# Recurrence gates and key products moved between ScalarE, VectorE and GpSimd in a two-layer hybrid backbone

## The chip, the cores and the metric

The kernel runs on one core of a Trainium2 chip. The metric is the device time of one execution in microseconds. Three runs of the kernel before took 1477.03, 1477.29 and 1481.97 us (median 1477.29 us). The engines are named as the profile names them: PE is TensorE, DVE is VectorE, ACT is ScalarE, POOL is GpSimd, SP issues the DMAs.

## The reference

Two layers work on 256 latent tokens `x` and 256 context tokens `ctx`, each 1024 wide, in fp32. A layer normalises, projects once, and feeds three mixers: a Fourier mix, windowed attention, and a gated linear recurrence that runs forward and backward over the tokens. The branches are gated, summed and projected, and a squared-ReLU MLP follows. What matters here is the recurrence. Cut to its core it computes, for 4 heads of 128 key channels:

```python
def hgrn_forget(z, lb):                 # gates of one direction
    k = (1.0 - lb) * sigmoid(-z)        # key
    f = sigmoid(z) + lb * sigmoid(-z)   # forget factor (the reference keeps its logarithm)
    return k, log(f)

def gla_chunked(q, k, v, logf, s0):     # o_t = q_t . S_t,  S_t = f_t * S_{t-1} + k_t v_t^T
    ...

def hgrn_bidir(q, kf, lff, kb, lfb, v, s_f, s_b):
    o_f, s_f_new = gla_chunked(q, kf, v, lff, s_f)
    o_b, s_b_new = gla_chunked(flip(q), flip(kb), flip(v), flip(lfb), s_b)
    return o_f + flip(o_b), s_f_new, s_b_new
```

With `lb` the lower bound, `f = (1 - lb) * sigmoid(z) + lb`: a sigmoid and an affine form with one factor and one summand per channel.

## The kernel before, in words

Large matrix products make up nearly all of PE's program. Weights arrive by DMA as tiles `raw` (128 x 1024 elements), are split into a high part `wh` (ACT, line 105) and a low part `wl` (DVE, line 108), and each product is done three times (`ws_group`, lines 275 to 277; `xs_group`, lines 291 to 293). The products of these lines need nothing of the recurrence until its branch is merged; between the recurrence's small products they are the fillers of PE's queue. The order on each engine is written by a scheduler when the program is built and stays fixed on the chip: an engine whose next instruction has to wait does not go on to a later one.

The recurrence is `hgrn(s, p)`, for the context (s = 0) and then the latent tokens (s = 1), and for two pairs of heads p, whose instructions alternate. Channels lie on partitions and the 256 tokens of two heads and both directions along the free axis. In the last layer the context has no queries and only makes its final states.

- The gates: `zt` holds the raw gates of both directions. ACT makes `sigmoid(-z)` into `wa` and `sigmoid(z)` in place. For each direction and head, line 877 (through `affine`, line 122) turns `zt` into the forget factors, 128 x 256 at a time, on DVE; lines 884 and following scale the keys into the tile `wk`, whose halves are `kop` and `ko`.
- The start of a pair: POOL multiplies the query with its sigmoid (line 890), DVE forms `wq` (the query times the factors, 128 x 1024), POOL forms a sum of keys (line 896), and PE makes the products inside a token (L866).
- A loop over h = 1, 2, 4, ..., 64, 128 joins neighbouring blocks of h tokens. At each level PE multiplies keys with queries (L866, L925 and L926 at the last), DVE masks the result into `cd`, multiplies the queries `wq` (line 931), and the keys are multiplied by the neighbouring block's decay. Up to h = 64 the keys of a pair take four instructions: two outer products into `wb` on DVE (lines 934 to 936, 128 x 128 each), a copy of the middle part on ACT (line 938), and one inner product on POOL (line 939, 128 x 256). `wb` and `wk` change places at each level. The next level's decays `z`, `t` are a product of this level's (line 948).
- For the context, PE then transposes the keys (L964) and multiplies them with the values (L973) into the states; L988 makes the output.

Of the kernel before, what the change touches and what calls it, by code (L numbers as in the profile page):

```python
# [15 lines left out]
AF = mybir.ActivationFunctionType  # L16
ALU = mybir.AluOpType
# [24 lines left out]
def _view(a, offset, dims):  # L42
    return bass.AP(tensor=a.tensor, offset=a.offset + offset, ap=[list(a.ap[0])] + [list(x) for x in dims])
# [3 lines left out]
def kernel(ctx: ExitStack, tc: tile.TileContext, io, dbg=None, stop=None):  # L47
    nc = tc.nc
# [11 lines left out]
    def sb(tag, shape, dtype=F32):  # L60
        uid[0] += 1
        return pool.tile(shape, dtype, tag=tag, name=f"{tag}{uid[0]}", bufs=BUFS[tag])

    def ps(tag, shape=(P, 512)):
        uid[0] += 1
        return psum.tile(list(shape), F32, tag=tag, name=f"{tag}{uid[0]}", bufs=PBUFS[tag])
# [7 lines left out]
    def act_cost(n):  # L74
        return 100 + 0.83 * n

    def dve_cost(n):
        return 70 + 1.04 * n

    def act(out, in_, func, cost=None, **kw):  # L80
        load["act"] += act_cost(out.free_size())
        return nc.scalar.activation(out=out, in_=in_, func=func, **kw)  # L82

    def tt(out, in0, in1, op):
        load["dve"] += dve_cost(out.free_size())
        return nc.vector.tensor_tensor(out=out, in0=in0, in1=in1, op=op)  # L86
# [5 lines left out]
    def evac(out, in_):  # L92
        n = out.free_size()
        top = max(load.values())
        for k in load:
            load[k] = max(load[k], top - 3000)
        if load["act"] + act_cost(n) < load["dve"] + dve_cost(n):
            load["act"] += act_cost(n)
            nc.scalar.copy(out=out, in_=in_)
        else:  # L100
            load["dve"] += dve_cost(n)
            nc.vector.tensor_copy(out=out, in_=in_)
# [18 lines left out]
    def affine(out, in_, mul, add):  # L121
        nc.vector.tensor_scalar(out=out, in0=in_, scalar1=mul, scalar2=add, op0=ALU.mult, op1=ALU.add)
# [292 lines left out]
    lbf = const.tile([P, DEPTH, 8], F32, name="lbf")  # L415
    oml = const.tile([P, DEPTH, 8], F32, name="oml")
# [148 lines left out]
    def layer(l):  # L565
# [278 lines left out]
        def hgrn(s, p):  # L844
# [4 lines left out]
            zt = z[s, p]  # L849
            k2 = sb("wk", [P, 2, 2, T])  # L850
            kop, ko = k2[:, 0], k2[:, 1]
            knew = sb("wb", [P, 2, T])
# [3 lines left out]
            def diag(c0, n):  # L856

                return _view(at, c0, [(512 + P, 2), (T, 2), (1, n)])

            def blocks(o, keys, n, queries):  # L860

                for j in range(2):
                    for hh in range(2):
                        for b in range(P // n):
                            t0 = j * P + b * n
                            nc.tensor.matmul(o[b * n:(b + 1) * n, j, hh, :], keys[:, hh, t0:t0 + n], queries(hh, t0, b),  # L866
                                             start=True, stop=True, tile_position=(0, b * n))
# [5 lines left out]
            for dr in range(2):  # L873
                for hh in range(2):
                    c = (1 - dr) * 4 + p * 2 + hh

                    affine(zt[:, dr, hh], zt[:, dr, hh], oml[:, l, c:c + 1], lbf[:, l, c:c + 1])
                    pair = sms[dr][:, hh].rearrange("p (n e) -> p n e", e=2)
                    if dr == 1:
                        outs = ((_view(k2, hh * T, [(2, P), (513, 2)]), pair),)  # L880
                    else:
                        outs = ((ko[:, hh, 0:T:2], pair[:, :, 0]), (kop[:, hh, 1:T:2], pair[:, :, 1]))
                    for o_, i_ in outs:
                        nc.vector.tensor_scalar(out=o_, in0=i_, scalar1=oml[:, l, c:c + 1], scalar2=None, op0=ALU.mult)
                        load["dve"] += dve_cost(128)
# [15 lines left out]
            tl, toff, n = zt, 0, 512  # L901
            t2l = sb("t2", [P, 2, 256])
            yield
            for li, h in enumerate(LEVELS + (128,)):
                nb = n // 2
                if doq and h < 32:
                    lv = ps("lv", (P, 2, 2, 32))
                    blocks(lv, kop, 32, lambda hh, t0, b: _view(q2, hh * T + t0, [(2 * h, 16 // h), (512 + h, 2), (1, h)]))
                    nc.vector.copy_predicated(cd, lmask[:, li, :].unsqueeze(1).unsqueeze(1).to_broadcast([P, 2, 2, 32]), lv)
                    load["dve"] += 200  # L910
                    if h == 16:
                        for b in range(4):
                            bs = slice(32 * b, 32 * b + 32)
                            nc.gpsimd.tensor_copy(out=diag(32 * b, 32)[bs], in_=cd[bs])
                elif doq and h < 128:

                    lv = ps("lv", (P, 2, 2, h))
                    blocks(lv, kop, h, lambda hh, t0, b: q2[:, 1 - b % 2, hh, t0 + (h, -h)[b % 2]:t0 + (2 * h, 0)[b % 2]])
                    for b in range(P // h):
                        bs = slice(h * b, h * b + h)  # L920
                        evac(diag(h * (b ^ 1), h)[bs], lv[bs])
                elif doq:
                    lv = ps("lv", (P, 2, 2, P))
                    for hh in range(2):
                        nc.tensor.matmul(lv[:, 0, hh, :], kop[:, hh, 0:P], q2[:, 1, hh, P:T], start=True, stop=True)  # L925
                        nc.tensor.matmul(lv[:, 1, hh, :], kop[:, hh, P:T], q2[:, 0, hh, 0:P], start=True, stop=True)  # L926
                    evac(_view(at, P, [(512 - P, 2), (T, 2), (1, P)]), lv)

                if doq and not (h == 128 and s == 0):
                    qv = _view(q2, 0, [(2 * h, nb), (512 + h, 2), (1, h)])  # L930
                    tt(qv, qv, _view(tl, toff + 1, [(2, nb), (n - 1, 2), (0, h)]), ALU.mult)
                if h < 128:
                    nq = nb // 2
                    for off, toff2 in ((0, n + 1), (3 * h, 2)):
                        tt(_view(knew, off, [(4 * h, nq), (1, h)]), _view(kop, off, [(4 * h, nq), (1, h)]),
                           _view(tl, toff + toff2, [(4, nq), (0, h)]), ALU.mult)
                    mid = [(4 * h, nq), (h, 2), (1, h)]
                    act(_view(knew, h, [(4 * h, nq), (1, 2 * h)]), _view(ko, h, [(4 * h, nq), (1, 2 * h)]), AF.Copy)
                    nc.gpsimd.tensor_tensor(out=_view(ko, h, mid), in0=_view(kop, h, mid),
                                            in1=_view(tl, toff, [(4, nq), (n + 3, 2), (0, h)]), op=ALU.mult)  # L940
                    kop, knew = knew, kop
                    if h == 1:
                        nt, noff = t2l, 0
                    elif h == 2:
                        nt, noff = zt, 0
                    else:
                        nt, noff = zt, toff + 2 * n
                    tt(_view(nt, noff, [(nb, 2), (1, nb)]), _view(tl, toff, [(n, 2), (2, nb)]),
                       _view(tl, toff + 1, [(n, 2), (2, nb)]), ALU.mult)
                    tl, toff, n = nt, noff, nb  # L950
                elif s == 0:
                    for off, toff2 in ((0, n + 1), (P, 0)):
                        kv_ = _view(kop, off, [(T, 2), (1, P)])
                        tt(kv_, kv_, _view(tl, toff + toff2, [(2, 2), (0, P)]), ALU.mult)
                yield
            dump(f"at{l}{s}{p}", at if doq else k2)
            if s == 0:
# [11 lines left out]
                for dr in range(2):  # L969
                    for hh in range(2):  # L970
                        c = (p * 2 + hh) * P
# [6 lines left out]
            if doq:  # L978
                o = ps("lv", (P, 2, 2, P))
                for i in range(2):  # L980
                    for hh in range(2):
                        c = (p * 2 + hh) * P
# [9 lines left out]
        for s in range(2):  # L992
            live = [hgrn(s, p) for p in range(2)]
            while live:
                live = [g for g in live if next(g, live) is not live]
# [378 lines left out]
```

## Time and profile before

| | |
|---|---|
| median of three runs | 1477.29 us |
| the profiled execution | 1479.77 us |
| its span in the trace | 1478.0 us |
| busy PE, DVE, ACT, POOL | 1442.6, 884.0, 663.9, 132.9 us |
| stretches of the recurrence, layer 0 | 215 to 262 us (context), 300 to 346 us (latent) |
| stretches of the recurrence, layer 1 | 1078 to 1112 us (context), 1112 to 1166 us (latent) |

A busy time is the sum over an engine's instructions on one execution. "PEclk" is the share of TensorE's full clock that was granted in a stretch: 1.00 is 2.4 GHz all the time, and a part of the stretch at 1.2 GHz lowers it. A wait is put down to the instruction that released it. The profiled execution took 1.8 us more than its span.

### The profile page before, as it was taken

To read this page: it belongs to the slowest core of one execution; us is meant where nothing else is said; L and a number is where in the kernel's file an instruction comes from. 1 tells how busy PE (TensorE), PEld (TensorE's weight loads), DVE (VectorE), ACT (ScalarE), POOL (GpSimd) and SP (SyncE) were. 2 spreads that over 40 slices of the span, in tenths; PEclk is the share of its full clock that TensorE was granted. 3 is DMA by queue.
4 is the path that set the end of the run, shared out by engine and by line. 5 is a ranking of instruction groups with operands and counts; after the bars stand their busy time and mean duration, and the time that the engine had idled before them with its cause. 6 is when DMAs were issued, how large, how long until landed. Compare 5 with 4: busy or idle time off the path is not lost.

```text
span 1478.0 us, 26336 instructions
## 1 busy us (share of the span) xinstructions
PE 1442.6 (98%) x10631; PEld 1253.1 (85%) x10632; DVE 884.0 (60%) x1783; ACT 663.9 (45%) x1220; POOL 132.9 (9%) x134
## 2 busy tenths in 40 slices
PE   7999998999999999999999999999998999999999
PEld 5887987888777788877777778998987999999998
DVE  4555759697334457433434334675788866766664
ACT  5454574454223346313223224464674545555544
POOL 3100003251000001000000000010055300000000
PEclk9999999999999999999999999999998999999999
DMA  9632212214466545455555533343223345656653
GB/s 309 223 95 63 72 58 69 73 42 132 159 214 199 171 129 158 141 166 174 173 169 173 171 114 101 87 119 100 61 81 102 115 143 174 197 159 199 187 184 115
DMA packets 178122, 205.83 MB, mean 139 GB/s; under 512 B 6800, under 2 KB 166320, under 8 KB 177488
## 3 DMA queue, kind: packets, MB, share of 16 engines
q1 hardware_dynamic: 177232, 201.44, 43.9%
q0 software_dynamic: 576, 2.62, 0.7%
q8 instruction: 83, 1.36, 0.4%
q14 instruction: 39, 0.32, 0.1%
q10 hardware_dynamic: 192, 0.08, 0.0%
HBM read 200.97 MB, written 3.15 MB: 138 GB/s over the span
## 4 chain that ended last, share of the span: by engine, by line
PE 83%; issue 8%; DVE 6%; POOL 1%; ACT 1%; SPq 1%; DMA 0%; DVEq 0%; ACTq 0%; POOLq 0%
PE mm L275 16%; PE mm L277 16%; PE mm L276 16%; PE tp L276 3%; PE tp L275 3%; PE tp L277 3%; PE lv L197 3%; PE lv L275 3%; PE lv L277 3%; PE lv L276 3%; PE mm L291 2%; PE mm L293 2%; PE mm L292 2%; DVE wq L86 1%; PE mm L512 1%
## 5 line engine op out<-in xcount | busy, mean ns | idle before, releaser
L86 DVE TENSOR_TENSOR wl<-raw,wh 128x1024 fp32r<-128x1024 f32 (+1 forms) x274 | 335.9, 1227 | 214.2 <-ACT wh L82 203.9
L82 ACT ACTIVATE wh<-raw 128x1024 fp32r<-128x1024 f32 (+1 forms) x278 | 290.3, 1047 | 350.0 <-PE mm L276 114.4
L275 PE MATMUL mm<-h,wh 128*128 128x512 f32 (+1 forms) x704 | 252.8, 359 | 1.3 <-DVE z L86 0.8
L277 PE MATMUL mm<-h,wl 128*128 128x512 f32 (+1 forms) x704 | 251.0, 357 | 1.9 <-DVE wl L86 1.9
L276 PE MATMUL mm<-h,wh 128*128 128x512 f32 (+1 forms) x704 | 250.5, 356 | 0.0
L275 PEld LDWEIGHTS mm<-h,wh 128*128 128x128 f32 x704 | 134.4, 191 | 34.6 <-ACT wh L82 6.7
L277 PEld LDWEIGHTS mm<-h,wl 128*128 128x128 f32 x704 | 134.4, 191 | 21.0 <-DVE wl L86 2.4
L276 PEld LDWEIGHTS mm<-h,wh 128*128 128x128 f32 x704 | 134.4, 191 | 19.3 <-issue 1.8
L291 PE MATMUL mm<-wh,h 128*128 128x256 f32 x384 | 112.2, 292 | 0.3 <-DVE xm L86 0.3
L293 PE MATMUL mm<-wh,h 128*128 128x256 f32 x384 | 110.6, 288 | 0.0
L292 PE MATMUL mm<-wl,h 128*128 128x256 f32 x384 | 109.6, 285 | 0.0
L275 PE MATMUL mm<-br,wh 128*128 128x258 f32 (+2 forms) x325 | 103.0, 317 | 0.2 <-DVE xm L86 0.2
L276 PE MATMUL mm<-br,wh 128*128 128x258 f32 (+2 forms) x325 | 103.1, 318 | 0.0
L277 PE MATMUL mm<-br,wl 128*128 128x258 f32 (+2 forms) x325 | 102.8, 317 | 0.0
L275 PE MATMUL mm<-z,wh 128*128 128x256 f32 (+1 forms) x272 | 89.0, 330 | 0.0
L276 PE MATMUL mm<-r,wh 128*128 128x256 f32 (+1 forms) x272 | 88.6, 327 | 0.0
L277 PE MATMUL mm<-z,wl 128*128 128x256 f32 (+1 forms) x272 | 88.4, 327 | 0.0
L90 DVE SCALAR_TENSOR_TENSOR xm<-mm,modT,xm 128x256 f32<-128x256 f32 x76 | 34.5, 480 | 76.5 <-PE mm L277 76.4
L291 PEld LDWEIGHTS mm<-wh,h 128*128 128x128 f32 x384 | 73.8, 192 | 1.2 <-DVE xm L86 0.4
L293 PEld LDWEIGHTS mm<-wh,h 128*128 128x128 f32 x384 | 74.0, 193 | 0.6 <-issue 0.3
L292 PEld LDWEIGHTS mm<-wl,h 128*128 128x128 f32 x384 | 73.9, 193 | 0.3
L82 ACT ACTIVATE g<-mm 128x512 f32<-128x512 f32 (+1 forms) x48 | 24.8, 516 | 102.5 <-PE mm L277 102.2
(363 smaller groups left out, 3123.2 us busy)
## 6 DMA issues: line engine op xcount, KB each, us to landing
raw<-in_w_ff SPq DMA_DIRECT2D x128, 512.0 KB, 4.1
raw<-in_w_in SPq DMA_DIRECT2D x106, 512.0 KB, 3.7
raw<-in_w_branch SPq DMA_DIRECT2D x24, 512.0 KB, 3.4
wa<-in_w_mod SPq DMA_DIRECT2D x24, 512.0 KB, 6.2
br<-in_w_mod SPq DMA_DIRECT2D x24, 512.0 KB, 5.7
wk<-in_w_mod SPq DMA_DIRECT2D x16, 512.0 KB, 4.5
wq<-in_w_mod SPq DMA_DIRECT2D x16, 512.0 KB, 6.4
raw<-in_w_out SPq DMA_DIRECT2D x16, 512.0 KB, 3.4
```

Of the source, the lines that this page charges most:

```text
L82: return nc.scalar.activation(out=out, in_=in_, func=func, **kw)
L86: return nc.vector.tensor_tensor(out=out, in0=in0, in1=in1, op=op)
L90: return nc.vector.scalar_tensor_tensor(out=out, in0=in0, scalar=scalar, in1=in1, op0=op0, op1=op1)
L197: nc.tensor.matmul(total[n][32 * j:32 * j + 32, :], cT[:, kt, :], raws[i][j // 2][:, j % 2, :], start=(kt == 0), stop=(kt == 7), tile_posi ...
L275: nc.tensor.matmul(o, w(0, kt, cs), act_h(kt)[:, c0:c1], start=(kt == 0), stop=False)
L276: nc.tensor.matmul(o, w(0, kt, cs), act_l(kt)[:, c0:c1], start=False, stop=False)
L277: nc.tensor.matmul(o, w(1, kt, cs), act_h(kt)[:, c0:c1], start=False, stop=(kt == nk - 1))
L291: nc.tensor.matmul(o, act_h(kt)[:, ts], w(0, kt, cs), start=(kt == 0), stop=False)
L292: nc.tensor.matmul(o, act_h(kt)[:, ts], w(1, kt, cs), start=False, stop=False)
L293: nc.tensor.matmul(o, act_l(kt)[:, ts], w(0, kt, cs), start=False, stop=(kt == 7))
L512: o = nc.tensor.matmul(sums[ch][t // 2][:, (t % 2) * T:(t % 2 + 1) * T], h[a_][d // 4][:, d % 4, ts], wt[ch, d // 4][w_][:, d % 4, :], sta ...
```

## The change

Three edits in `hgrn`. The affine form of the gates becomes an ACT activation (Identity with a factor and a summand per partition) in place of DVE's tensor_scalar. The two outer key products of a level become one DVE instruction of 128 x 256, whose views take the first and last block of each four. The inner key product goes from POOL to DVE.

```diff
-                    affine(zt[:, dr, hh], zt[:, dr, hh], oml[:, l, c:c + 1], lbf[:, l, c:c + 1])
+                    act(zt[:, dr, hh], zt[:, dr, hh], AF.Identity, scale=oml[:, l, c:c + 1], bias=lbf[:, l, c:c + 1])
...
-                    for off, toff2 in ((0, n + 1), (3 * h, 2)):
-                        tt(_view(knew, off, [(4 * h, nq), (1, h)]), _view(kop, off, [(4 * h, nq), (1, h)]),
-                           _view(tl, toff + toff2, [(4, nq), (0, h)]), ALU.mult)
+                    ends = [(4 * h, nq), (3 * h, 2), (1, h)]
+                    tt(_view(knew, 0, ends), _view(kop, 0, ends), _view(tl, toff + n + 1, [(4, nq), (1 - n, 2), (0, h)]), ALU.mult)
                     mid = [(4 * h, nq), (h, 2), (1, h)]
                     act(_view(knew, h, [(4 * h, nq), (1, 2 * h)]), _view(ko, h, [(4 * h, nq), (1, 2 * h)]), AF.Copy)
-                    nc.gpsimd.tensor_tensor(out=_view(ko, h, mid), in0=_view(kop, h, mid),
-                                            in1=_view(tl, toff, [(4, nq), (n + 3, 2), (0, h)]), op=ALU.mult)
+                    tt(_view(ko, h, mid), _view(kop, h, mid), _view(tl, toff, [(4, nq), (n + 3, 2), (0, h)]), ALU.mult)
```

In the program, 32 tensor_scalars leave DVE and 32 activations come to ACT; 112 outer products become 56; 56 inner products leave POOL and come to DVE. The scheduler also writes other orders around them. Line numbers behind the edit are smaller by 2, so that L964 of before is L962 of the change.

First place, PE at the start of layer 0's recurrence. `tp` from `a` is the end of the attention; `lv` from `r` and `t` are the products inside a token, `lv` from `wq` and `wk` those of the first level, and `mm` the large products. Before:

```order
L803 MATMUL tp_1698<-a_1612,a_797 64x128 x8
L803 MATMUL tp_1698<-a_1655,a_797 64x128
L866 MATMUL lv_2376<-r_1721,t_2374 32x32 x9
L803 MATMUL tp_1698<-a_1655,a_797 64x128 x7
L866 MATMUL lv_2376<-r_1721,t_2374 32x32 x7
L866 MATMUL lv_2419<-r_1721,t_2417 32x32 x16
L866 MATMUL lv_2439<-wq_2372,wk_2353 32x32 x16
L866 MATMUL lv_2463<-wq_2415,wk_2396 32x32 x16
```

With the change, where the line of dots leaves out 23 more large products:

```order
L803 MATMUL tp_1698<-a_1612,a_797 64x128 x8
L803 MATMUL tp_1698<-a_1655,a_797 64x128
L866 MATMUL lv_2376<-r_1721,t_2374 32x32 x16
L277 MATMUL mm_3471<-h_101,wl_3442 128x512
...
L277 MATMUL mm_3509<-h_101,wl_3506 128x512
L803 MATMUL tp_1698<-a_1655,a_797 64x128 x7
L866 MATMUL lv_2419<-r_1721,t_2417 32x32 x16
L866 MATMUL lv_2439<-wq_2372,wk_2353 32x32 x16
L866 MATMUL lv_2462<-wq_2415,wk_2396 32x32 x16
```

25 large products of 512 columns now stand between the first pair's products inside a token and the first level's.

Second place, DVE at the same start; `z_1717` and `z_1718` are the gates of the two pairs, `wk_2353` and `wk_2396` their keys. Before:

```order
L884 TENSOR_SCALAR wk_2396<-wa_2398,oml 128x128x2 x2
L122 TENSOR_SCALAR z_1717<-z_1717,oml,lbf 128x256 x4
L122 TENSOR_SCALAR z_1718<-z_1718,oml,lbf 128x256 x4
L86 TENSOR_TENSOR wb_2354<-wk_2353,z_1717 128x128 x2
L86 TENSOR_TENSOR wb_2397<-wk_2396,z_1718 128x128 x2
L86 TENSOR_TENSOR wq_2372<-r_1721,z_1717 128x1024
L86 TENSOR_TENSOR wl_3592<-raw_3589,wh_3591 128x1024
L86 TENSOR_TENSOR wq_2415<-r_1721,z_1718 128x1024
```

With the change:

```order
L884 TENSOR_SCALAR wk_2396<-wa_2398,oml 128x128x2 x2
L86 TENSOR_TENSOR wq_2372<-r_1721,z_1717 128x1024
L86 TENSOR_TENSOR wb_2354<-wk_2353,z_1717 128x128x2
L86 TENSOR_TENSOR wk_2353<-wk_2353,z_1717 128x128x2
L86 TENSOR_TENSOR wb_2397<-wk_2396,z_1718 128x128x2
L102 COPY cd<-lv_2376 128x128
L86 TENSOR_TENSOR t_2395<-z_1717 128x512
L86 TENSOR_TENSOR wl_3564<-raw_3561,wh_3563 128x1024
L86 TENSOR_TENSOR wk_2396<-wk_2396,z_1718 128x128x2
L86 TENSOR_TENSOR wq_2415<-r_1721,z_1718 128x1024
```

The eight affine instructions are gone, the first `wq` stands at the head, and the inner key products (`wk` from `wk`) stand among the rest.

Third place, PE in layer 1 where the context's keys are transposed for the states (`tp` from `ident` and `wb` or `wk`). Before:

```order
L275 MATMUL mm_10964<-h_8497,wh_10960 128x256
L276 MATMUL mm_10964<-h_8499,wh_10960 128x256
L277 MATMUL mm_10964<-h_8497,wl_10961 128x256
L964 MATMUL tp_10303<-ident,wb_10196 128x128
L964 MATMUL tp_10303<-ident,wk_10195 128x128
```

With the change:

```order
L277 MATMUL mm_11044<-br_9009,wl_11027 128x256
L275 MATMUL mm_11044<-br_9009,wh_11026 128x256
L276 MATMUL mm_11044<-br_9010,wh_11026 128x256
L962 MATMUL tp_10261<-ident,wb_10168 128x128
L962 MATMUL tp_10261<-ident,wk_10167 128x128
```

The transposes moved behind 99 more large products of 256 columns, from the gates' products (`h`) into those of the first merged branch (`br`).

## Rows read from the trace of the kernel before

**Rows 1.** The page, part 1: busy us, share, count of each engine.
```profile
PE 1442.6 (98%) x10631; PEld 1253.1 (85%) x10632; DVE 884.0 (60%) x1783; ACT 663.9 (45%) x1220; POOL 132.9 (9%) x134
```

**Rows 2.** By stretch: length, busy PE, PEld, DVE, ACT, POOL (count), PEclk, DMA, GB/s.
```profile
215.00:262.00 47.00, 42.03 (x520) 33.83 (x518) 41.24 (x88) 23.19 (x42) 15.42 (x14) 0.93 0.25 77
300.00:346.00 46.00, 41.45 (x723) 38.34 (x722) 45.58 (x117) 23.27 (x62) 24.50 (x24) 0.96 0.19 55
1078.00:1112.00 34.00, 27.73 (x233) 26.10 (x231) 32.75 (x76) 22.06 (x41) 23.87 (x13) 0.99 0.32 95
1112.00:1166.00 54.00, 48.74 (x758) 46.37 (x759) 48.52 (x95) 23.79 (x43) 25.09 (x25) 0.91 0.40 116
```

**Rows 3.** PE's waits, 215 to 346 us: us in total, times, longest.
```profile
PE lv L866 <- DVE wq L86: 6.3, 5, 2.6
PE lv L866 <- DVE cd L102: 2.4, 1, 2.4
```

**Rows 4.** PE's waits, 1078 to 1180 us.
```profile
PE tp L964 <- POOL wk L939: 3.4, 1, 3.4
PE lv L866 <- DVE wq L86: 2.8, 4, 1.0
PE mm L277 <- DVE wl L86: 1.9, 2, 1.1
```

**Rows 5.** The chain that ended last, 1094 to 1114 us: start, us, what.
```profile
1097.83 14.31 POOL wk L939 x6
```

**Rows 6.** PE in order of time, 242 to 247 us: start, us, instruction.
```profile
242.31 0.63 PE L276 MATMUL mm<-h,wh 128*128 128x512 f32 x1
242.74 0.63 PE L277 MATMUL mm<-h,wl 128*128 128x512 f32 x1
...
245.24 0.39 PE L276 MATMUL mm<-h,wh 128*128 128x512 f32 x1
245.47 0.39 PE L277 MATMUL mm<-h,wl 128*128 128x512 f32 x1
```

**Rows 7.** Line 939 alone, whole span: length, busy POOL (count), PEclk, DMA, GB/s.
```profile
0.00:1478.00 1478.00, 73.50 (x56) 0.99 0.45 139
```

**Rows 8.** Line 939's instructions by form: ns min/median/max, first and last start.
```profile
L939 POOL TENSOR_TENSOR wk<-wk,z x32: 613/998/6094, 230.6 to 1167.6; 128x256 f32<-128x256 f32 x32
```

**Rows 9.** DVE in order of time: four pieces of both layers.
```profile
228.01 5.36 DVE L122 TENSOR_SCALAR z<-z,oml,lbf 128x256 f32<-128x256 f32 x8
...
236.37 1.21 DVE L86 TENSOR_TENSOR wq<-r,z 128x1024 f32<-128x1024 f32 x1
...
1080.21 2.67 DVE L122 TENSOR_SCALAR z<-z,oml,lbf 128x256 f32<-128x256 f32 x8
...
1128.65 4.31 DVE L86 TENSOR_TENSOR wq<-r,z 128x1024 f32<-128x1024 f32 x2
```

**Rows 10.** POOL in order of time, 1127 to 1133 us.
```profile
1127.61 2.27 POOL L896 TENSOR_TENSOR t<-wk 128x512 f32<-128x512 f32 x1
1129.96 1.93 POOL L939 TENSOR_TENSOR wk<-wk,z 128x256 f32<-128x256 f32 x1
```

**Rows 11.** DVE in order of time: products of other sizes and levels.
```profile
284.31 1.09 DVE L86 TENSOR_TENSOR wb<-wb,z 128x256 f32<-128x256 f32 x3
...
1138.26 1.15 DVE L86 TENSOR_TENSOR wq<-wq,z 128x512 f32<-128x512 f32 x1
...
1150.33 0.68 DVE L86 TENSOR_TENSOR wq<-wq,z 128x512 f32<-128x512 f32 x1
1150.93 0.48 DVE L86 TENSOR_TENSOR wk<-wb,z 128x128 f32<-128x128 f32 x2
```

**Rows 12.** ACT grouped, with a summand per partition: count | busy us, mean ns.
```profile
L82 ACT ACTIVATE g<-g,beta 128x256 f32<-128x256 f32 x34 | 16.9, 500 | 0.6 <-DVE g L86 0.5
```

**Rows 13.** ACT in order of time, layer 0's start.
```profile
228.04 0.63 ACT L82 ACTIVATE t<-r 128x512 f32<-128x512 f32 x1
229.04 0.45 ACT L82 ACTIVATE wb<-wk 128x256 f32<-128x256 f32 x1
```

## What the change is expected to do

> **What bounds the kernel.** I read the page's busy times first, then the stretches of the recurrence, PE's waits in them, and last the rows of single instructions for prices. PE is busy 1442.6 us of 1478 [rows 1], so an edit on other engines can only give back what PE loses to waits, and to the slower clock that follows them. In the four stretches of the recurrence, length less PE's busy time is 4.97, 4.55, 6.27 and 5.26 us [rows 2], together 21.0 us. There the granted clock falls as well: (1 - 0.93) x 47 + (1 - 0.96) x 46 + (1 - 0.99) x 34 + (1 - 0.91) x 54 = 3.3 + 1.8 + 0.3 + 4.9 = 10.3 us of full-clock time missing [rows 2]. What that does is seen behind the two waits of 2.6 and 2.4 us at layer 0's start [rows 3]: the products of 512 columns start 0.43 us apart, and later 0.23 us apart [rows 6], which is 1.2 against 2.4 GHz. Some of the slow time lies in a wait and costs nothing; I take off 1.8 us, half of the 2.4 us wait and of about 1.2 us of the 3.4 us wait of rows 4. So at most 21.0 + 8.5 = 29.5 us are to be had.
>
> Who is late? In layer 0 it is DVE, with `wq` (6.3 us in five waits) and `cd` (2.4 us) [rows 3]; in layer 1 POOL's inner key product (3.4 us in one wait) and `wq` again (2.8 us) [rows 4]. DVE itself is full: 45.58 of 46 us and 48.52 of 54 us in the latent stretches, 32.75 of 34 in layer 1's context [rows 2]. And one run of six POOL products holds 14.31 us of the chain ahead of layer 1's transposes [rows 5].
>
> DVE is full partly with waiting for POOL. Eight affine instructions took 5.36 us at layer 0's start and 2.67 us in layer 1 [rows 9]; the two `wq` at 1128.65 took 4.31 us, where one at 236.37 took 1.21 [rows 9], while POOL worked at lines 896 and 939 [rows 10]. POOL suffers as well: its 56 inner products take 73.5 us [rows 7], where the shortest needs 0.613 [rows 8].
>
> **The change, part by part.**
> *DVE gains work.* 56 inner products of 128 x 256: three instructions of that size took 1.09 us [rows 11], some 0.33 each without the overlap of neighbours. 56 x 0.33 = 18.5 us. At h = 1 the views go in steps of single elements; there `wq` took 1.15 us against 0.68 at a later level [rows 11], so the eight products of that level may cost up to double: +2.6.
> *DVE loses work.* Two outer products took 0.48 us, 0.20 each without overlap [rows 11]; 112 x 0.20 = 22.4 becomes 56 x 0.33 = 18.5, minus 3.9. The eight fewer instructions per start, 32 x 0.33 alone (2.67 us by eight [rows 9]), take off 10.6. The merged instruction's jump between outer blocks is in no row; between no saving at all and 3.9, I take 3.9, since inner runs of the same lengths stand in the 0.20 us ones.
> *Net on DVE, POOL left aside:* 18.5 + 2.6 - 3.9 - 10.6 = +6.6 us.
> *DVE no longer blocked.* What a POOL product cost DVE is not a row of its own. Below it is nothing (the products that DVE sat beside while it waited anyway); above it is POOL's whole busy time, 73.5 us. The nearest rows, 4.31 - 2 x 1.13 (1.21 less 0.08 of overlap) = 2.0 us lost by the pair of `wq` beside two POOL instructions, and 2.7 us lost by eight affines, lie around one short product's own length. I take 56 x 0.61 = 34 us at most and three quarters of it, 25 us, as the value, because DVE is full in three of the four stretches and seldom idle beside POOL. Lines 890 and 896 stay on POOL and go on blocking at each start. So DVE ends some 18 us lighter (25 - 6.6), between 27 lighter and 6.6 heavier.
>
> The Trainium skill's page "SBUF — State Buffer", section "Who interferes with whom", says that VectorE and GpSimd share one pair of ports as an exclusive lock, which an instruction of VectorE with two inputs from SBUF needs whenever GpSimd reads. By it the lost time is the other's whole length; the 4.31 us pair agrees, and the sum would sit at the full 34 us instead of 25. It is the case for the first rival below.
>
> *ACT gains work.* 32 activations of 128 x 256 with factor and summand per partition. One with a summand alone takes 0.500 us [rows 12]; above that, a plain one of 128 x 512 takes 0.63 [rows 13]. I take 0.50, the same size, for 16 us in all (up to 20), 4 us per start. ACT is busy 23.2 of 47 and about as little in the other stretches [rows 2], so it has the room. But its queue is in order: at layer 0's start the affines stand behind the first copy `wb` of 229.04 [rows 13], so the first pair's gates are ready near 229.5 + 2.0 = 231.5 and the second's, one evacuation later, near 234, where DVE finished both at 228.01 + 5.36 = 233.4 [rows 9]. The first pair gains 2 us, the second loses half a one. In that time DVE can only do what needs no gates. What is behind the affines on ACT are the splits `wh`, up to 4 us later at each start; they are cover that must hold, and the products that read them stand a whole weight tile ahead.
>
> The page "ScalarE: Activation LUTs" of the Trainium skill, section "Rules for kernel authors", would have multiplications and additions on VectorE and not on ScalarE, against this edit. What leaving costs VectorE less is by the skill's page "VectorE: DVE Perf Modes", section "The perf-mode tier table" (a tensor_scalar in fp32 at twice the rate) and its section "The TRN2 errata — SBUF-src ops pay a fixed extra latency per instruction" (a measured fixed part of about 150 cycles), an estimated (150 + 128) / 0.96 = 290 ns, so that 32 x 0.29 = 9.3 us would be freed and not 10.6. The trace's 2.67 us by eight says 0.33; the row decides, and the sum stays.
>
> *POOL loses* 73.5 us [rows 7], and with it a hand-over to another engine in each level: ACT's copy is now followed by DVE, which also makes the outer product. The 3.4 us wait for POOL [rows 4] and the 14.31 us [rows 5] have no source left.
>
> *PE's order.* At layer 0's start 25 large products now stand ahead of the first level: 25 x 0.23 = 5.7 us of work where PE waited 2.6 + 2.4 us [rows 3]. The second `wq` must be ready by then: from 234 on, DVE has about 4 us of other instructions ahead of it, so near 239, and PE comes to it near 241. In layer 1 the transposes move behind 99 products of 256 columns, at 27.73 us by 233 [rows 2] 0.12 us each, some 12 us; DVE's keys come earlier, not later. What ends later in turn are the recurrence's outputs, which are wanted only at the last branch.
>
> *Sum.* Gone: layer 0's context 5.0 us of waits and 2 of slow clock; layer 1's context 6.3 and most of 3. For the latent stretches (4.55 + 5.26 us, and 3.5 of clock) I don't take all. There DVE keeps 14 + 14 inner products: in 300 to 346 us 45.6 + 5.2 - 1.0 - 2.6 - 8.5 = 38.7 us of DVE work stand against 46 - 4.55 - 1.8 = 39.6 us of PE's, too near to leave no wait. I leave 6 of the 13.3 us there. That gives 29.5 - 6 = 23.5 us. The profiled execution's own time, 1479.8 us (1.8 over its span), would be 1456.3; it lies 2.5 above the median of the runs, and against the median of 1477.3 the sum is 1453.8, said as 1454.
>
> **The rivals.**
> *All of it.* If every GpSimd product blocked DVE for its length, the latent stretches run free too: 1477.3 - 29.5 = 1447.8. For it: the pair of `wq`. Against: 38.7 beside 39.6 us.
> *DVE stays the bound, half the gain.* If blocking was worth only the 7 to 12 us that make up for the added work, the waits for `wq` and `cd` (6.3 + 2.4 + 2.8) mostly stay, and only those for POOL (3.4 us, some 3 of clock) and the context starts' reorder (5 us) go: about 11 us, 1466. For it: DVE's 99% in 300 to 346 us.
> *Nothing to see.* The order of PE moves the waits behind the recurrence, to the merge that reads its output, or the split `wh` behind ACT's 4 us of affines makes PE wait as long as before at each start: within 7.4 us, 1475. Against: ACT's half-idle stretches.
> *Slower, by DVE in the latent stretches.* 28 inner products there add 9.2 + 1.3 us, the merge takes off 2, and only layer 0 has its affines inside (2.6): +5.9 us net. If a POOL product blocked DVE by less than 5.9 / 28 = 0.21 us on average, each level takes longer than before, PE waits those 6 us more, and slow clock behind the waits adds about 3: 1486. Rows 9 speak against so little.
>
> **How the numbers follow.** The likeliest case, 1450 to 1460, has 0.52; all of it 0.14; half 0.18; nothing 0.09; slower 0.07. The range reaches from under the full gain, 1446, to past the half, 1470, and leaves out the last two. This kernel's runs tell 0.5% (7.4 us) from no change. Faster by more than that: 0.52 + 0.14 and 0.16 of the half case, 0.82; within: 0.11; slower: 0.07.
>
> **What would show it.** PE's wait for POOL at the state transposes gone; the two waits of 2.6 and 2.4 us at layer 0's start gone, and no 1.2 GHz behind them; PEclk 0.98 or more in the latent stretches; DVE's eight-instruction groups free of doubled lengths except beside lines 890 and 896; DVE's 128 x 256 products near 0.33 us and ACT's affines near 0.5. The forecast is wrong if PE's idle time in the four stretches stays over 12 us, or if PE waits for `wl` more than the 1 or 2 us of before.

## The result, and the profile after

The change takes 1454.62 us (median of five, 1454.15 to 1455.25), against 1477.79 us for the kernel before (median of five): the ratio is 0.9833, 95% interval 0.982 to 0.9846, which is 24.7 us less (23.2 by the two medians). The prediction said 1454. The profiled execution took 1454.62 us over a span of 1452.8.

First the page's busy times after, to be set beside [rows 1].

```profile
PE 1433.9 (99%) x10632; PEld 1247.3 (86%) x10632; DVE 863.1 (59%) x1751; ACT 676.2 (47%) x1252; POOL 64.8 (4%) x78
```

PE did the same products in 8.7 us less: that is the slow clock that went (its mean over the span rose from 0.993 to 0.999). The span fell by 25.2 us, so the other 16.5 us were waits. DVE, which took over 56 products and gave up 32 affines and 56 outer products, is busy 20.9 us less.

The four stretches of the recurrence, moved to where they now lie (columns as in [rows 2]):

```profile
215.00:262.00 47.00, 47.00 (x553) 38.06 (x550) 39.34 (x86) 29.12 (x52) 5.96 (x4) 1.00 0.29 88
295.00:341.00 46.00, 44.34 (x749) 41.35 (x748) 45.70 (x117) 29.93 (x78) 8.93 (x11) 1.00 0.21 60
1070.00:1104.00 34.00, 34.00 (x295) 33.50 (x295) 28.14 (x59) 29.60 (x58) 0.00 (x0) 1.00 0.50 146
1104.00:1158.00 54.00, 50.82 (x804) 48.38 (x802) 52.66 (x115) 28.71 (x64) 13.01 (x12) 0.97 0.41 118
```

In both context stretches (first and third row) PE is busy from end to end at the full clock. In the latent ones 1.66 and 3.18 us of waits are left, and one piece at 0.97. DVE is still full there: 45.70 of 46 and 52.66 of 54 us.

PE's waits after, from 215 to 345 us, which answer to [rows 3]:

```profile
PE lv L866 <- DVE wq L86: 1.2, 1, 1.2
PE tp L1067 <- DVE g L86: 0.5, 2, 0.3
```

and from 1060 to 1170 us, which answer to [rows 4]:

```profile
PE lv L866 <- DVE wq L86: 1.9, 1, 1.9
PE mm L291 <- DVE xm L86: 0.6, 1, 0.6
PE lv L866 <- DVE cd L102: 0.4, 1, 0.4
PE lv L866 <- POOL t L896: 0.3, 1, 0.3
```

The wait of 3.4 us for POOL's product at the transposes is gone, and so are both waits at layer 0's start. PE's wait for `wl` of 1.9 us is gone too.

What the new instructions took: ACT's four affines of each pair at layer 0's start, with the first copy `wb` ahead of them, an evacuation `xm` between and the copy `a` behind (compare [rows 13]; the dots leave out three instructions):

```profile
229.24 0.45 ACT L82 ACTIVATE wb<-wk 128x256 f32<-128x256 f32 x1
229.57 2.07 ACT L82 ACTIVATE z<-z,lbf,oml 128x256 f32<-128x256 f32 x4
231.54 0.58 ACT L82 ACTIVATE xm<-mm 128x512 f32<-128x512 f32 x1
232.02 2.07 ACT L82 ACTIVATE z<-z,lbf,oml 128x256 f32<-128x256 f32 x4
...
235.78 0.57 ACT L99 COPY a<-tp 128x512 f32<-128x512 f32 x1
```

That is 0.52 us each, and gates ready at 231.64 and 234.09 (231.5 and 234 were predicted). DVE's products of 128 x 256 in layer 1, one at h = 1 and three at a late level:

```profile
1122.48 0.62 DVE L86 TENSOR_TENSOR wk<-wk,z 128x256 f32<-128x256 f32 x1
...
1136.28 0.41 DVE L86 TENSOR_TENSOR wk<-wb,z 128x256 f32<-128x256 f32 x1
1136.61 0.41 DVE L86 TENSOR_TENSOR wk<-wk,z 128x256 f32<-128x256 f32 x1
1136.95 0.42 DVE L86 TENSOR_TENSOR wk<-wb,z 128x256 f32<-128x256 f32 x1
```

The three start 0.33 to 0.34 us apart (a row shows 0.41 because neighbours overlap by 0.08); the one at h = 1 takes 0.62. These are the prices that the sum used.

### The profile page after: what moved, and what is told of

Read it like the earlier page. It is cut to its first block, busy times and chain, and to the rows that moved or that the text cites. A ratio compares the mean times of both kernels' runs of the same rounds, so it can differ in the third digit from the quotient of the medians.

```text
span 1452.8 us, 26188 instructions
## 1 busy us (share of the span) xinstructions
PE 1433.9 (99%) x10632; PEld 1247.3 (86%) x10632; DVE 863.1 (59%) x1751; ACT 676.2 (47%) x1252; POOL 64.8 (4%) x78
## 4 chain that ended last, share of the span: by engine, by line
PE 95%; DVE 3%; issue 1%; SPq 1%; DMA 0%; ACT 0%; ACTq 0%; DVEq 0%
PE mm L275 18%; PE mm L276 17%; PE mm L277 17%; PE tp L276 3%; PE tp L275 3%; PE tp L277 3%; PE lv L275 3%; PE lv L277 3%; PE lv L197 3%; PE lv L276 3%; PE mm L291 3%; PE mm L293 3%; PE mm L292 3%; PE tp L803 2%; PE mm L512 1%; PE tp L796 1%
```

## The experiments

Three theories stood against each other. Mine: POOL's products held DVE's instructions up, DVE was the late engine, and relieving it ends the waits. Rival 1: the new order of PE, which the scheduler wrote around the edits, is the gain. Rival 2: POOL's product was simply late in the chain of the levels. Differences below are of medians; the ratios, each to runs of the kernel before made beside it, give the same within 1 us unless said otherwise.

| kernel | us (median) | ratio to before, 95% interval | DVE busy us | POOL busy us |
|---|---|---|---|---|
| before | 1477.79 to 1479.93 | 1 | 884.0 | 132.9 |
| the change | 1454.62 | 0.9833 (0.982 to 0.9846) | 863.1 | 64.8 |
| inner product alone | 1466.10 | 0.9913 (0.99 to 0.9927) | 878.6 | 66.7 |
| affine alone | 1462.59 | 0.989 (0.9874 to 0.9905) | 871.1 | 113.3 |
| merge alone | 1475.10 | 0.9974 (0.9964 to 0.9983) | 877.6 | 131.9 |
| change without inner product | 1463.31 | 0.9895 (0.9881 to 0.9908) | 864.8 | 119.9 |
| change without affine | 1462.37 | 0.989 (0.9874 to 0.9907) | 874.2 | 68.1 |
| change without merge | 1455.33 | 0.984 (0.9822 to 0.9857) | 866.6 | 71.1 |
| change, idle products on POOL | 1469.25 | 0.993 (0.9917 to 0.9942) | 881.5 | 120.6 |
| change, PE's old order at one place | 1460.67 | 0.9872 (0.9857 to 0.9887) | 864.3 | 64.6 |
| before, PE's new order at that place | 1473.04 | 0.9957 (0.9944 to 0.9969) | 882.3 | 137.4 |
| change without affine, new order edge | 1463.75 | 0.99 (0.9883 to 0.9917) | 873.4 | 65.8 |
| the same, recurrence's products off POOL | 1453.11 | 0.9829 (0.9811 to 0.9848) | 869.2 | 45.0 |
| change, recurrence's products off POOL | 1450.88 | 0.9806 (0.9792 to 0.9819) | 862.0 | 43.8 |

**One edit at a time.** The inner product alone:

```diff
-                    nc.gpsimd.tensor_tensor(out=_view(ko, h, mid), in0=_view(kop, h, mid), in1=..., op=ALU.mult)
+                    tt(_view(ko, h, mid), _view(kop, h, mid), ..., ALU.mult)
```

> The kernel before with one of the three edits: the inner key product on VectorE. Theory (VectorE is held up by GpSimd's products, so taking them away pays for the 21 us of work that VectorE gains): VectorE's busy time falls by some 4 us, PE's wait for POOL at the state transposes is gone, those for wq at the starts stay, because the affine forms still stand there: about 1466 us (1461 to 1471). Rival 1 (the new order of PE, with 25 large products ahead of the first level, is the gain): that order comes only with the affine edit, so 1474 or more. Rival 2 (GpSimd's product was late in the chain of the levels, and nothing else matters): nearly all of the gain, 1456 to 1459.

It took 1466.1 us. DVE does 56 products more (21.1 us by the sum's price) and is busy 5.4 us less, so by that price some 26.5 us of DVE's time had been POOL's doing. At layer 0's start PE goes on waiting, now for POOL's sum of keys (3.3 us) and for `cd` (1.3), and not for `wq` as I expected. The affine alone:

```diff
-                    affine(zt[:, dr, hh], zt[:, dr, hh], oml[:, l, c:c + 1], lbf[:, l, c:c + 1])
+                    act(zt[:, dr, hh], zt[:, dr, hh], AF.Identity, scale=oml[:, l, c:c + 1], bias=lbf[:, l, c:c + 1])
```

> The kernel before with the affine form of the gates on ScalarE alone. Theory: VectorE loses 10.6 us of work (2.6 per start), GpSimd goes on holding it up: the two waits at layer 0's start are mostly gone, those in the latent stretches and for POOL at the transposes stay: about 1466 us (1461 to 1471). Rival 1 (PE's order): most of the gain, 1456 to 1460. Rival 2 (GpSimd late in the chain): within 3 us of before, 1474 or more.

1462.6 us: more of a gain than the 1466 I expected, less than Rival 1 did. From 215 to 262 us PE doesn't wait at all; in the latent stretches it waits as before. One part of the expectation missed: PE's wait of 3.4 us for POOL at layer 1's transposes is gone, though POOL still makes the inner products (more on this below). The merge alone:

```diff
-                    for off, toff2 in ((0, n + 1), (3 * h, 2)):
-                        tt(_view(knew, off, [(4 * h, nq), (1, h)]), ...)
+                    ends = [(4 * h, nq), (3 * h, 2), (1, h)]
+                    tt(_view(knew, 0, ends), _view(kop, 0, ends), ...)
```

> The kernel before with the outer products of a level as one instruction alone. Theory: 56 instructions fewer on VectorE, 3.9 us of its work, with GpSimd's product now next to one long instruction: about 1474 us (1471 to 1477). Both rivals: within 2 us of before.

1475.1 us, as the theory had it. By their ratios the three alone give 12.9 + 16.3 + 3.8 = 33 us, more than the 24.7 of all three: they end the same waits twice over, and there were only 29.5 us to be had.

**One edit taken back.** The change with POOL's inner product again (the first diff reversed):

> The kernel with the change, but its inner key product back on GpSimd (affine form on ScalarE and one outer product stay). Theory: GpSimd holds VectorE up again, some 20 us of VectorE's time, of which the affine and the merge take back 14.5: PE waits in the latent stretches and for POOL at layer 1's transposes: 1463 us (1459 to 1468). Rival 1 (PE's order, which this kernel nearly shares with the change): 1454 to 1457. Rival 2 (GpSimd late in the chain): 1468 or more, as all of the gain hangs on this edit.

1463.3 us. PE's order at layer 0's start is the change's, and elsewhere close to it, and still 8.7 us are lost, so Rival 1 falls as the whole story; some 15.5 of the 24.7 us stay without this edit, so Rival 2 falls too. PE's waits in this kernel, 215 to 1170 us, the three longest:

```profile
PE lv L866 <- DVE wq L86: 4.3, 5, 2.5
PE lv L866 <- DVE cd L102: 1.8, 1, 1.8
PE lv L925 <- DVE wq L86: 1.4, 2, 1.0
```

They are waits for DVE, not for the product that went back to POOL; the wait for POOL at the transposes, which I expected back, did not come. The change with the affine form back on DVE, and the change with two outer products again (the other diffs reversed):

> The kernel with the change, but the gates' affine form back on VectorE (one outer product and the inner product on VectorE stay). PE's order at layer 0's start is then that of before. Theory that the affine edit's gain is in two parts, PE's order at layer 0's start (6 us, as the two runs on the order had it) and VectorE's load in the other three places (up to 10 us of VectorE's time, little of it on the path now that GpSimd doesn't hold VectorE up): 1462 us (1459 to 1465). Rival (VectorE's 10.6 us of work are the gain, and all of it is on the path): 1465 to 1469.

> The kernel with the change, but the outer products of a level as two instructions again (affine on ScalarE and inner product on VectorE stay). VectorE gains 56 instructions and 3.9 us of work, where the latent stretches have little room: 1457 us (1455 to 1460). Rival (VectorE has room now, nothing waits for these): 1454 to 1455.

1462.4 and 1455.3 us. Without the affine edit PE waits at layer 0's start again (3.2 us for POOL's `t`, 1.5 for `cd`). Without the merge DVE is busy 3.5 us more (3.9 was the price), but the time is only 0.7 us over the change, and the intervals overlap. It lies in the theory's range (1455 to 1460) and 0.3 us above the rival's, so this run doesn't tell them apart; it does bound the merge's worth behind the other two edits.

**Does POOL hold DVE up?** A product that nobody reads, at each level, in the change (its output tile is bf16, and the cuts are marked):

```diff
+        idle = const.tile([P, T], BF16, ...)
...
                     tt(_view(ko, h, mid), _view(kop, h, mid), ..., ALU.mult)
+                    lev = _view(tl, toff, [(4, nq), (n + 3, 2), (0, h)])
+                    nc.gpsimd.tensor_tensor(out=_view(idle, 0, [(2 * h, nq), (h, 2), (1, h)]), in0=lev, in1=lev, op=ALU.mult)
```

> The kernel with the change, and beside every inner key product on VectorE a product of the same size on GpSimd (decays by decays, 128 x 256) into a tile that nobody reads. PE, VectorE and ScalarE have the change's own orders, so only GpSimd's work is added, 56 instructions. Theory (GpSimd's instructions hold VectorE's up): VectorE's busy time rises by 15 to 25 us, PE waits in the latent stretches and the context ones again: about 1465 us (1460 to 1471). Rival (GpSimd's products cost only because their results came late): nobody waits for these results, so 1454 to 1456.

1469.25 us, 14.6 more than the change. This is the cleanest of the pairs, because PE, DVE and ACT run the same instructions in the same order as in the change. Its busy times:

```profile
PE 1439.0 (98%) x10631; PEld 1251.1 (85%) x10632; DVE 881.5 (60%) x1751; ACT 676.2 (46%) x1252; POOL 120.6 (8%) x134
```

DVE needs 18.4 us more for its same 1751 instructions, with 55.8 us of POOL's work beside it; ACT's 676.2 haven't moved. Layer 0's start, DVE in this kernel:

```profile
233.35 1.73 DVE L86 TENSOR_TENSOR wq<-r,z 128x1024 f32<-128x1024 f32 x1 [3.38 <-ACT z L82]
235.00 1.73 DVE L86 TENSOR_TENSOR wb<-wk,z 128x256 f32<-128x256 f32 x1
236.65 1.14 DVE L86 TENSOR_TENSOR wk<-wk,z 128x256 f32<-128x256 f32 x1
237.71 1.76 DVE L86 TENSOR_TENSOR wb<-wk,z 128x256 f32<-128x256 f32 x1
```

and POOL beside it:

```profile
233.33 0.67 POOL L941 TENSOR_TENSOR idle<-z 128x256 bf16<-128x256 f32 x1 [1.48 <-ACT z L82]
233.96 2.27 POOL L897 TENSOR_TENSOR t<-wk 128x512 f32<-128x512 f32 x1
236.19 1.09 POOL L941 TENSOR_TENSOR idle<-z 128x256 bf16<-128x256 f32 x1
237.25 1.71 POOL L891 TENSOR_TENSOR r<-r,t 128x512 f32<-128x512 f32 x1
```

The same instructions in the change:

```profile
231.75 1.23 DVE L86 TENSOR_TENSOR wq<-r,z 128x1024 f32<-128x1024 f32 x1 [3.35 <-ACT z L82]
232.89 1.73 DVE L86 TENSOR_TENSOR wb<-wk,z 128x256 f32<-128x256 f32 x1
234.53 0.64 DVE L86 TENSOR_TENSOR wk<-wk,z 128x256 f32<-128x256 f32 x1
235.09 0.65 DVE L86 TENSOR_TENSOR wb<-wk,z 128x256 f32<-128x256 f32 x1
```

Three of these DVE products take 0.5 to 1.1 us more with a POOL instruction beside them (1.73 for 1.23, 1.14 for 0.64, 1.76 for 0.65); the first `wb` is long in both kernels, and in both POOL's sum of keys runs beside it. Later in the kernel most of the lengthened ones take some 0.4 us more (0.83 for 0.42). Not all of the 14.6 us is this: the useless products also stand in POOL's queue ahead of `t` and `r`, and PE waits 1.5 us for `t`, DVE 1.2.

The Trainium skill's page "SBUF — State Buffer", section "Who interferes with whom", has VectorE and GpSimd share ports as an exclusive lock. The lengths of these pairs agree: the inner `wk` lost 0.50 us where the POOL product beside it had 0.63 still to run, the second `wb` 1.11 us where it had 1.25. Over the whole kernel the price was 18.4 / 56 = 0.33 us per product, about half of the shortest product's 0.61 us, although DVE was at work beside every one of the 56. The other half fell on POOL: its useless products took 0.98 us on the mean, 0.37 more than the shortest.

**Is it PE's order at layer 0's start?** The second `wq` of the context, before and after:

```profile
238.64 1.21 DVE L86 TENSOR_TENSOR wq<-r,z 128x1024 f32<-128x1024 f32 x1
```

```profile
239.09 1.22 DVE L86 TENSOR_TENSOR wq<-r,z 128x1024 f32<-128x1024 f32 x1
```

It ends at 239.85 before and at 240.31 after: not earlier. What changed is when PE asks for it:

```profile
240.92 0.91 PE L866 MATMUL lv<-wq,wk 128*32 128x32 f32 x64
```

So two kernels differ from change and before, in their text, by this order alone: in the first, 24 large products are queued behind the first level, in the second the first level behind them. The scheduler answers with small moves on other queues: in the first, thirteen instructions of DVE and ACT between 239 and 273 us, in the second some 110 between 238 and 375 us, so the first is the cleaner of the two.

```diff
+                    if l == 0 and c == 3 and b == 0:
+                        with tc.issue_after(first_lv[1]):
+                            gate(wg, b, mv(c * 2 + b))
...
```

> The kernel with the change, but with PE's old order at one place: the 24 large products of one gate group are queued behind the first level of layer 0's context, as before; the engines' work is the change's. Theory that the order is the gain at this place (the second wq ends at 240.3 us in the change and at 239.9 us before, so it is not earlier): PE waits some 5 us there again and runs at the lower clock behind it, some 2 us: 1461 us (1458 to 1463). Rival, as the sum of the prediction has it (VectorE is lighter, so the wait goes whatever the order): 1454 to 1456.

```diff
-                    gate(wg, b, mv(c * 2 + b))
+                    o = gate(wg, b, mv(c * 2 + b))
+                    if l == 0 and c == 3 and b == 0:
+                        for i in first_lv[0]:
+                            tc.add_manual_dep(i.ins, last_mm[0].ins.name, ...)
```

> The kernel before with nothing of the change but PE's new order at the same place: the first level of layer 0's context is queued behind the 24 large products of that gate group. Theory that the order is the gain there: 5.0 us of waits and 2 of slow clock go: about 1471 us (1468 to 1473). Rival (VectorE's load): within 2 us of before, 1476 to 1479, the wait moved to the next level.

1460.67 us, 6.05 over the change; and 1473.04, 6.4 under before (by the ratio, 4.6 to 8.3), 0.04 past the end of its range. Both are near the order's numbers and far from the rivals'. PE's waits from 230 to 245 us in the first:

```profile
PE tp L803 <- ACT a L99: 2.2, 1, 2.2
PE lv L867 <- DVE wq L86: 2.1, 1, 2.1
```

The first of them is new, and it is the price of the affine edit that the order hides: the copy `a` of the attention's last transposes stands behind eight affines in ACT's queue (235.78 us in the rows of ACT above, 231.78 before). In the second kernel PE waits at that start for no more than 0.6 us, though DVE and POOL do all the work of before.

**The same order without the affine edit.** The change with the affine back on DVE and the second order edge:

> The same kernel (the change with the affine form on VectorE) and the first level of layer 0's context queued behind the 24 large products, as the change has it. Theory of the order: the start's waits of layer 0 go without any affine on ScalarE: 6 us under the kernel without this edge, 1456 us (1453 to 1459). Rival (VectorE's load): within 2 us of the kernel without this edge.

This one failed: 1463.75 us, no better than 1462.4 without the edge, as the rival said. PE's wait from 230 to 245 us was no longer where the edge was:

```profile
PE lv L868 <- POOL t L898: 3.2, 1, 3.2
```

It is for the second pair's products inside a token, which the edge leaves where they were. Why POOL is late, POOL and then DVE in this kernel:

```profile
232.08 4.86 POOL L892 TENSOR_TENSOR r<-r,t 128x512 f32<-128x512 f32 x1 [1.64 <-ACT t L82]
236.90 1.26 POOL L898 TENSOR_TENSOR t<-wk 128x512 f32<-128x512 f32 x1
```

```profile
231.81 0.63 DVE L86 TENSOR_TENSOR wb<-wk,z 128x256 f32<-128x256 f32 x1
232.36 0.63 DVE L86 TENSOR_TENSOR wk<-wk,z 128x256 f32<-128x256 f32 x1
232.91 0.63 DVE L86 TENSOR_TENSOR wb<-wk,z 128x256 f32<-128x256 f32 x1
233.46 1.22 DVE L86 TENSOR_TENSOR wq<-r,z 128x1024 f32<-128x1024 f32 x1
234.60 1.22 DVE L86 TENSOR_TENSOR wl<-raw,wh 128x1024 fp32r<-128x1024 f32 x1
236.97 2.27 DVE L86 TENSOR_TENSOR wq<-r,z 128x1024 f32<-128x1024 f32 x1 [1.15 <-POOL r L892]
```

Five DVE products without a gap, of ordinary lengths, run from 231.81 to 235.82 us; POOL's product, some 1.3 us long elsewhere, lies beside them all and ends 1.12 us after the last. The holding-up goes the other way here, and DVE then waits for the very result. The same product took 5.01 us with the inner product alone and 4.85 in the change without affine, ahead of PE's waits of 3.3 and 3.2 us for POOL's `t` there. Whether this, and not the load of the affine, is what remained, the next kernel was to test: the same, with POOL's last products in the recurrence on DVE.

```diff
-                nc.gpsimd.tensor_tensor(out=q, in0=q, in1=sg, op=ALU.mult)
+                tt(q, q, sg, ALU.mult)
...
-                nc.gpsimd.tensor_tensor(out=ks, in0=kop, in1=ko, op=ALU.add)
+                tt(ks, kop, ko, ALU.add)
```

> The kernel with the affine form on VectorE and PE's order edge, and the recurrence's last twelve products of GpSimd on VectorE too. If moving the affine form to ScalarE is worth only PE's order once GpSimd is out of VectorE's way, this is within 2 us of the version without GpSimd's products that keeps the affine on ScalarE (1450.9): 1451 to 1453. If VectorE's 10.6 us of work count by themselves: 1455 to 1461.

1453.11 us, 10.6 less, just over the first forecast and short of the second, and PE doesn't wait at layer 0's start. The test is not clean: the sum of keys is ready at 235.70 us there (238.16 without this edit), and the scheduler also put 12 large products ahead of PE's need for it, where PE would otherwise have come at 234.6. Not all of the 10.6 us is this start, where 3.2 were lost: POOL's last products also leave DVE alone in the latent stretches.

**A better version.** The same last diff on the change itself:

> The kernel with the change, and the recurrence's last products on GpSimd (the query by its sigmoid, the sum of keys, 128 x 512, twelve in all) on VectorE as well. Theory (GpSimd's instructions hold VectorE's up): VectorE gains 12 x 0.65 = 8 us of work and loses about as much of being held up; the wait of 0.3 us for the sum of keys goes; some of the 4.5 us of PE's waits that the change left in the latent stretches goes with it: 1453 us (1450 to 1457). Rival (VectorE is the bound there and has no room): 1458 or more.

1450.88 us, 3.7 under the change; the two intervals don't touch. DVE does twelve instructions more and is busy 862.0 us, 1.1 less than in the change. Its four stretches:

```profile
215.00:262.00 47.00, 47.00 (x554) 38.00 (x551) 39.42 (x91) 28.98 (x52) 0.00 (x0) 1.00 0.28 88
295.00:341.00 46.00, 45.18 (x767) 42.26 (x765) 45.02 (x121) 30.75 (x81) 4.68 (x8) 1.00 0.21 60
1070.00:1104.00 34.00, 34.00 (x294) 33.51 (x291) 28.32 (x60) 29.05 (x57) 0.00 (x0) 1.00 0.48 144
1104.00:1158.00 54.00, 52.77 (x840) 50.05 (x839) 52.73 (x121) 31.21 (x67) 4.62 (x8) 1.00 0.40 116
```

0.8 and 1.2 us of waits are left of the recurrence's 21, at the full clock. Against the kernel just above (1453.11), which keeps the affine on DVE, ACT's affines are worth some 2.2 us (3.4 by the ratios, whose intervals overlap) once POOL is out of the way and the order is right.

## Why the prediction was right

*The bound.* 29.5 us were said to be had, 23.5 were forecast, and the profiled execution fell by 25.2 (1479.8 to 1454.6). In the four stretches the waits went from 21.0 to 1.66 + 3.18 = 4.84 us, the clock's loss from 10.3 to (1 - 0.97) x 54 = 1.6. In the latent stretches that is 4.84 + 1.6 = 6.4 us left, where the sum left 6. That 6 was a judgement ("too near to leave no wait"), so its nearness is partly luck. The 1.8 us taken off for slow time inside waits are not seen: PE's busy time fell by 8.7 us, all of the clock's 10.3 - 1.6. One sign was missed, the clock of 0.98 in the latent stretches (0.97 in layer 1); the others that the traces can show came.

*DVE's own work.* Merge: 3.5 us of DVE against 3.9. Products of 128 x 256: 0.33 us, and 0.62 at h = 1, as priced. Affine: DVE's busy time differs by 874.2 - 863.1 = 11.1 us with and without it, against 10.6.

*DVE no longer blocked.* 25 us were taken, between 0 and 34. The runs give 26.5 (before against inner product alone), 22.8 (864.8 + 21.1 - 863.1, change without inner product against the change) and 18.4 (idle products, the only pair with DVE's order unchanged). The rival of the full 34 us falls, and so does that of 7 to 12.

*ACT.* 0.52 us against 0.50, and the times of both pairs' gates to 0.1 us. What the step missed is who stands behind the affines: it named the splits `wh`, and it was the copy `a`, worth 2.2 us where PE's order doesn't cover it.

*PE's order.* The 5.7 us of large products where PE had waited, and the second `wq` near 239 with PE there near 241, came as 240.31 and 240.92: the margin was 0.6 us, not 2. The sum took this start's 7 us as one term, and the two order runs put 6.05 and 6.4 us of it on the order alone. The wait for the second `wq` is not DVE's lighter load: that `wq` isn't earlier. But the order needs the rest to be on time: in the change without affine it brought nothing, as PE waited there for POOL's sum of keys.

*Layer 1's transposes.* The prediction gave their wait of 3.4 us to POOL's inner product, with "no source left". The traces show that there is more to it. That product was itself held up: it is the one of 6.09 us [rows 8], beside DVE products that follow one another without a gap from 1106.02 to 1111.66 us (before; the POOL row holds two products, of which PE waits for the first):

```profile
1106.04 6.67 POOL L939 TENSOR_TENSOR wk<-wk,z 128x256 f32<-128x256 f32 x2
1109.31 2.35 DVE L86 TENSOR_TENSOR wl<-raw,wh 128x1024 fp32r<-128x1024 f32 x2
```

And the wait is also gone in the two kernels that have the affine on ACT and keep the inner product on POOL; in both the scheduler put the transposes behind 66 to 68 more large products than before (some 100 in the change). It stays, 3.4 us for POOL or 2.3 for DVE, in the two that leave the transposes' place about as before (PE's new order, merge alone). Nor did the keys get quicker. From the context's first `sigmoid(-z)` to the end of its last key product it is 37.7 us before (1075.05 to 1112.71) and 41.25 in the change:

```profile
1062.30 2.20 ACT L82 ACTIVATE wa<-z 128x512 f32<-128x512 f32 x4
1102.79 0.76 DVE L86 TENSOR_TENSOR wb<-wb,z 128x256 f32<-128x256 f32 x2
```

PE comes to the transposes at 1103.83 us, 0.3 us behind the last of them. So the later place of the transposes may have ended this stretch's 6.3 us of waits by itself, or together with POOL's relief; no run pins that place, and the share of each is open.

Of the 24.7 us that the change brings, about 6 are thus shown to be the scheduler's, which moved fillers ahead at layer 0's start and only with the affine on ACT (its order puts the 24 products there, or most of them, in each kernel above whose affine is on ACT, and in none whose affine is on DVE, unless an edge forces it). Some 6 more, in layer 1's context, may be. The two latent stretches gave some 10 (16.5 us of waits and slow clock before, 6.4 after). There DVE's load and POOL's holding it up count: with the idle products, at the change's own order, PE's waits rise from 1.66 to 5.83 us in layer 0's latent stretch (1.5 of it for POOL's own late `t`) and from 3.18 to 5.49 in layer 1's. DVE's load and the holding-up end the same waits and can't be added up one by one.

*The rivals.* "All of it" (1447.8) needs DVE free in the latent stretches; it was not, and even the better version ends 3 us above. "Slower" needed a POOL product to cost DVE under 0.21 us; it cost 0.33 to 0.47 (18.4 and 26.5 over 56).

## What to carry to other kernels

An instruction on an otherwise idle engine isn't free if it makes the busy one longer: compare the length of the same instruction with and without a neighbour on the other engine before work is put there. When a scheduler orders the queues, test its order apart from the edit, by pinning the one place that moved: 6 us of this gain needed no faster engine, and some 6 more may hang on a second place that no run pinned. And edits that shorten the same waits don't add up: 33 us one by one were 24.7 together.

## What the runs showed of the hardware that was not expected

Holding up went both ways. DVE's products were lengthened by POOL's (1.73 us for 1.23), but DVE products in a row also kept a POOL product of some 1.3 us going for 4.86 us, until DVE's queue paused. The kernel before has the same in its longest single wait: a POOL product that takes 0.61 us at its shortest lasted 6.09 us beside 5.6 us of DVE's work without a gap, and ended 0.47 us after it. So POOL's lateness, too, was in part DVE's doing. The other unexpected number is how even an engine's time stays beside this: ACT was busy 676.2 us with and without 55.8 us more of POOL's work.
